# Final norm bound behind the activations of the last expert, its stores on GpSimd's queue, and six way-down pieces multiplied unsplit

## The chip, the core and the metric

One core of a Trainium2 chip runs the whole program. The metric is the device time of one execution in microseconds (us); lower is better. The kernel before was timed three times: median 2451.87 us (2450.3 to 2453.91).

## The reference

Two transformer blocks are computed in float32 on 1024 tokens of width D = 1024. Only the end of the second block matters here: an expert-choice feed-forward layer, its scatter back into the rows, and a last rmsnorm.

```
def expert_choice_ffn(h, w_router, w_gate, w_up, w_down):
    cap = EC_CAPACITY_FACTOR * n // N_EXPERTS            # 128 of 1024 tokens
    aff = jax.nn.softmax((h @ w_router), axis=-1)
    g, idx = lax.top_k(jnp.swapaxes(aff, 1, 2), cap)     # each of 16 experts picks its tokens
    xs = jax.vmap(lambda hb, ib: hb[ib])(h, idx)
    a = jnp.einsum('becd,edf->becf', xs, w_gate)
    u = jnp.einsum('becd,edf->becf', xs, w_up)
    y = jnp.einsum('becf,efd->becd', silu(a) * u, w_down) * g[..., None]
    out = jax.ops.segment_sum(y.reshape(-1, d), flat, num_segments=bsz * n)
...
x = x + gt2 * expert_choice_ffn(h2, w_router, w_gate, w_up, w_down)
return rmsnorm_2(x, g_final)      # x * rsqrt(mean(x*x) + EPS) * g_final
```

A token may be picked by several experts, so the rows of x are complete only when every expert that holds them has been added.

## The kernel before

**The expert stage.** It is the last 600 us. Sixteen experts e (0 to 15) are each cut into four quarters c4, which makes 64 steps i = 4e + c4. A step needs two gate/up pieces of the weights (called gu 2i and gu 2i+1 here) and one way-down piece (d i), 1 MB each. `pipelined` runs three stages one step apart: `ex_gu(s)`, the gate/up products and the silu; `ex_T(s-1)`, the transposes of the 128x256 activation; `ex_down(s-2)`, the way-down products into `py`, which gathers an expert's 128 rows over its four steps.

**Split products.** A float32 weight half is split into two parts: ACT casts it (`wh`, L1521) and DVE subtracts (`wl`, L1522). Each product is then three matmuls (`mm3`, L187 to L189). One step has 24 of them for gate/up and 12 for way-down. Where `whole` is true (before: i = 63 alone) the way-down product is one float32 matmul on the weight as it was loaded (L1741, two records each, eight in a step), with no cast, no `wl`, and a plain copy `af` in place of `ah` and `al`.

**Weights in a ring.** The loaded weights live in 17 slots of 1 MB. `raw_tile` (L1479) walks over the slots' pools in a fixed turn; a pool has 1, 2 or 4 slots. A slot can be loaded again once the last `wl` of its old weight is done on DVE. All loads go through SP's queue, in the order in which the program's scheduler put them; a load that waits holds up all behind it. Each engine works through its own queue in the same way.

**Rows and the final norm.** When an expert's four steps are done, its rows `ys` are scaled by the gate and `gt2` and added into `x3_d` in DRAM by an indirect DMA of GpSimd (L1752). Behind the scatter of expert 14 the last three way-down pieces are loaded (held back by the small copies of L1498), then `final_rows` (L1757) loads `g_final` (`gfin`) and all of x3 in eight tiles of 128 rows (`x3t`, two in a slot), squares them on ACT (`jk`, L168), takes the power on GpSimd (`rrstd`, L164), scales on DVE (L1777) and stores on SP's queue (L1778). The rows of expert 15 are gathered first (`xg`, L1765), get their last addition and norm at the very end (L1788 to L1795), and overwrite their places in `out` by an indirect DMA of GpSimd (L1796), which waits for all other stores.

**What sets the order.** The program is written in the order above; a scheduler that simulates the engines then decides each queue's order and which slot of a pool a tile gets. `tc.issue_after(x)` keeps what is written in it behind instruction x.

Of the kernel before, what the change touches and what calls it, by code (L numbers as in the profile page):

```python
# [6 lines left out]
F32 = mybir.dt.float32  # L7
# [53 lines left out]
ONORM = (26, 29)  # L61
MORE = 2
XSB = 3
LASTN = 3
OH = 1
KV0 = 1
D1S = 3
# [27 lines left out]
def tile_two_blocks(ctx, tc, A, out):  # L95
# [1574 lines left out]
    with TP(name="exg", bufs=2, space=PSUM) as psg, \  # L1670
# [12 lines left out]
        def ex_gu(i, _):  # L1683
# [20 lines left out]
            if c4 == 3 and e + 1 < NE:  # L1704
                x_T(e + 1)
            sg = ex.tile([P, 2, P], F32, name="sg", tag="sg").rearrange("p j c -> p (j c)")
            nc.scalar.activation(sg, pg[:, 0:256], AF.Silu)
            nc.vector.tensor_tensor(out=sg, in0=sg, in1=pg[:, 256:512], op=ALU.mult)
            return sg

        def ex_T(i, ac):
            whole = i == 4 * NE - 1
            pT = pst.tile([P, 4, P], F32, name="pT", tag="tp")
            for j in range(2):
                nc.tensor.transpose(pT[:, j, :], ac[:, j * P:(j + 1) * P], ident)
            if whole:
                af = ex.tile([P, 2, P], F32, name="af", tag="sg")
                nc.scalar.copy(af, pT[:, 0:2, :])
                return af, None
            ah = exa.tile([P, 2, P], F32R, name="ah", tag="ah")  # L1720
            al = exb.tile([P, 2, P], F32R, name="al", tag="al", bufs=ALB)
            split(ah, al, pT[:, 0:2, :])
            return ah, al

        def ex_down(i, a):
            e, c4 = divmod(i, 4)
            whole = i == 4 * NE - 1
            ah, al = a
            if c4 == 0:
                pys[e] = psy.tile([P, D], F32, name="py", tag="y")  # L1730
# [28 lines left out]
        def final_rows():  # L1759

            i_ = ROWS.index("g_final_2")
            last["g"] = ex.tile([P, D], F32, name="gfin", tag="xs", bufs=XSB)
            nc.sync.dma_start(last["g"], A["rows"][i_:i_ + 1, :].partition_broadcast(P).rearrange("p o n -> p (o n)"))
            last["x"] = ex.tile([P, D], F32, name="xg", tag="xs", bufs=XSB)
            nc.gpsimd.indirect_dma_start(out=last["x"], out_offset=None, in_=x3_d,  # L1765
                                         in_offset=bass.IndirectOffsetOnAxis(ap=xT[NE - 1][2], axis=0))
            for u in range(NT // 2):
                xt = raw_tile("x3t")
                for j in range(2):
                    t = 2 * u + j  # L1770
                    x3 = xt[:, j * D:(j + 1) * D]
                    nc.sync.dma_start(x3, x3_d[trow(t), :])
                    jk = ex.tile([P, D], BF16, name="jk", tag="hot", bufs=1)
                    ss = stat.tile([P, 1], F32, name="ss", tag="ss")
                    sumsq(x3, ss, jk)
                    r = rstd_of(ss, 1, D)
                    nc.vector.scalar_tensor_tensor(out=x3, in0=x3, scalar=r, in1=last["g"], op0=ALU.mult, op1=ALU.mult)  # L1777
                    nc.sync.dma_start(out[trow(t), :], x3)  # L1778
# [5 lines left out]
        sq = stat.tile([P, 2], F32, name="ssl", tag="ssl")  # L1784
        jk = ex.tile([P, D], BF16, name="jk", tag="hot", bufs=1)
        for nh in range(2):
            c = slice(nh * 512, nh * 512 + 512)
            nc.vector.scalar_tensor_tensor(out=ys[:, c], in0=pys[NE - 1][:, c], scalar=xT[NE - 1][3], in1=gt2[:, c],  # L1788
                                           op0=ALU.mult, op1=ALU.mult)
            nc.vector.tensor_tensor(out=ys[:, c], in0=ys[:, c], in1=last["x"][:, c], op=ALU.add)  # L1790
            sumsq(ys[:, c], sq[:, nh:nh + 1], jk[:, c])
        ss = stat.tile([P, 1], F32, name="ss", tag="ss")
        nc.vector.tensor_tensor(out=ss, in0=sq[:, 0:1], in1=sq[:, 1:2], op=ALU.add)
        r = rstd_of(ss, 1, D)
        nc.vector.scalar_tensor_tensor(out=ys, in0=ys, scalar=r, in1=last["g"], op0=ALU.mult, op1=ALU.mult)  # L1795
        nc.gpsimd.indirect_dma_start(out=out, out_offset=bass.IndirectOffsetOnAxis(ap=xT[NE - 1][2], axis=0),  # L1796
                                     in_=ys, in_offset=None)
    for p in reversed(exs):
        p.release()
    rt_pool.release()  # L1800
# [109 lines left out]
```

## Time and profile before

| | us |
|---|---|
| median of 3 runs | 2451.87 (2450.3 to 2453.91) |
| the profiled execution | 2454.56 |
| its span, first to last instruction | 2452.6 |
| TensorE (PE) busy | 2322.0 (95%) |
| VectorE (DVE) busy | 1612.5 (66%) |
| ScalarE (ACT) busy | 1122.5 (46%) |
| GpSimd (POOL) busy | 600.1 (24%) |
| mean granted TensorE clock | 0.978 |

The profiled execution is 1.96 us longer than its span and 2.69 us over the median. Matmul records overlap by some 0.17 us, so the start-to-start distance of two, 0.23 us, is what a 128x512 product takes on PE.

### The profile page before, as it was taken

The numbers are of one execution on the slowest core, as the hardware profiler recorded it, in microseconds if no ns is written. First come the engines' busy times: TensorE is split into PE (matmuls) and PEld (weight loads), VectorE is DVE, ScalarE is ACT, GpSimd is POOL, SyncE is SP. The second block draws the span as 40 slices with busy tenths as digits, with TensorE's granted clock in tenths as the row PEclk, the third lists the DMA queues.
The fourth block names the chain that finished last, engine by engine and source line by source line (L and its number), as shares of the span: only waits on it lengthen the run. The fifth ranks groups of instructions, "written<-read, shape, count | busy, mean of one in ns | idle before, by whom it ended". The sixth has DMA issues, their size and how long they took to land. (4 is left out here: it accounts for less than half of the span.)

```text
span 2452.6 us, 33977 instructions
## 1 busy us (share of the span) xinstructions
PE 2322.0 (95%) x12875; PEld 1872.4 (76%) x12875; DVE 1612.5 (66%) x2554; ACT 1122.5 (46%) x1932; POOL 600.1 (24%) x597
## 2 busy tenths in 40 slices
PE   7999999999999999999997999999949999999996
PEld 7977787787878878788876988666737888877774
DVE  4265666457686665554557842575378999999887
ACT  4254566343321222222223421453237887877775
POOL 1100540130000000000005400263154565565512
PEclk9999999999999999999999999999979999999998
DMA  6111003225243331111115320014679999999975
GB/s 199 30 44 61 24 27 98 94 102 163 83 155 103 121 104 61 52 52 43 46 58 141 92 65 26 26 40 147 239 280 337 383 382 381 397 367 360 369 256 214
DMA packets 111031, 381.66 MB, mean 156 GB/s; under 512 B 12215, under 2 KB 19224, under 8 KB 94484
## 3 DMA queue, kind: packets, MB, share of 16 engines
q1 hardware_dynamic: 98980, 344.99, 38.8%
q0 software_dynamic: 6416, 22.97, 4.0%
q10 hardware_dynamic: 5472, 11.54, 1.2%
q8 instruction: 101, 1.65, 0.3%
q14 instruction: 62, 0.51, 0.1%
HBM read 340.08 MB, written 39.37 MB: 155 GB/s over the span
## 5 line engine op out<-in xcount | busy, mean ns | idle before, releaser
L1522 DVE TENSOR_TENSOR wl<-raw,wh 128x1024 fp32r<-128x1024 f32 x380 | 473.9, 1284 | 45.6 <-ACT wh L1521 40.0
L1521 ACT CAST wh<-raw 128x1024 fp32r<-128x1024 f32 x382 | 391.5, 1051 | 67.6 <-PE pg L189 33.7
L171 ACT CAST wh<-raw 128x512 fp32r<-128x512 f32 (+1 forms) x177 | 107.5, 641 | 411.5 <-PE psu L188 225.7
L187 PE MATMUL psu<-hT_hi,wh 128*128 128x512 f32 x704 | 278.6, 396 | 5.8 <-ACT wh L171 5.5
L188 PE MATMUL psu<-hT_lo,wh 128*128 128x512 f32 x704 | 277.8, 395 | 0.0
L189 PE MATMUL psu<-hT_hi,wl 128*128 128x512 f32 x704 | 276.7, 394 | 0.2 <-DVE wl L172 0.2
L164 POOL TENSOR_TENSOR rrstd<-vrstd,neghalf 128x1 f32<-128x1 f32 x51 | 36.1, 730 | 866.5 <-DVE vrstd L161 866.4
L172 DVE TENSOR_TENSOR wl<-raw,wh 128x512 fp32r<-128x512 f32 (+1 forms) x177 | 124.0, 729 | 148.1 <-ACT wh L171 147.9
L888 DVE TENSOR_TENSOR ffn_y<-ffn_y,psd 128x512 f32<-128x512 f32 x160 | 108.6, 684 | 158.0 <-PE psd L189 157.8
L187 PE MATMUL pg<-wh,xh 128*128 128x512 f32 x512 | 204.8, 400 | 5.2 <-ACT xh L171 5.2
L1539 POOL TENSOR_SCALAR hot<-iota,slot 128x128 bf16<-128x128 f32 x112 | 201.2, 2529 | 17.6 <-PE pi L1547 13.2
L188 PE MATMUL pg<-wl,xh 128*128 128x512 f32 x512 | 204.2, 399 | 0.3 <-DVE wl L1522 0.3
L189 PE MATMUL pg<-wh,xl 128*128 128x512 f32 x512 | 202.4, 395 | 0.0
L187 PEld LDWEIGHTS psu<-hT_hi,wh 128*128 128x128 f32 x704 | 133.0, 189 | 38.2 <-ACT wh L171 8.4
L189 PEld LDWEIGHTS psu<-hT_hi,wl 128*128 128x128 f32 x704 | 133.0, 189 | 31.5 <-DVE wl L172 1.1
L188 PEld LDWEIGHTS psu<-hT_lo,wh 128*128 128x128 f32 x704 | 133.1, 189 | 29.9
L187 PE MATMUL psd<-wh,acth 128*128 128x512 f32 x352 | 139.9, 398 | 3.3 <-DVE ffn_y L888 2.6
L188 PE MATMUL psd<-wl,acth 128*128 128x512 f32 x352 | 139.1, 395 | 0.0
L189 PE MATMUL psd<-wh,actl 128*128 128x512 f32 x352 | 138.1, 395 | 0.0
L187 PEld LDWEIGHTS pg<-wh,xh 128*128 128x128 f32 x512 | 96.6, 189 | 25.8 <-ACT xh L171 7.1
L188 PEld LDWEIGHTS pg<-wl,xh 128*128 128x128 f32 x512 | 96.7, 189 | 24.5 <-DVE wl L1522 5.7
L189 PEld LDWEIGHTS pg<-wh,xl 128*128 128x128 f32 x512 | 96.5, 189 | 18.9
(497 smaller groups left out, 5390.0 us busy)
## 6 DMA issues: line engine op xcount, KB each, us to landing
raw<-in_w_gu SPq DMA_DIRECT2D x128, 1024.0 KB
raw<-in_w_down SPq DMA_DIRECT2D x64, 1024.0 KB
wa<-in_w_ada SPq DMA_DIRECT2D x48, 512.0 KB
raw<-in_w_up SPq DMA_DIRECT2D x88, 256.0 KB
raw<-in_w_down SPq DMA_DIRECT2D x44, 256.0 KB
raw<-in_w2t SPq DMA_DIRECT2D x36, 256.0 KB
xt<-in_x SPq DMA_DIRECT2D x16, 512.0 KB
wor<-in_w_out SPq DMA_DIRECT2D x32, 256.0 KB
```

Of the source, the lines that this page charges most:

```text
L164: nc.gpsimd.tensor_tensor(out=r, in0=v, in1=neghalf[:, :n], op=ALU.pow)
L171: nc.scalar.copy(hi, src)
L172: nc.vector.tensor_tensor(out=lo, in0=src, in1=hi.bitcast(F32), op=ALU.subtract)
L187: nc.tensor.matmul(ps, lh, rh, start=start, stop=False)
L188: nc.tensor.matmul(ps, lh, rl, start=False, stop=False)
L189: return nc.tensor.matmul(ps, ll, rh, start=False, stop=stop)
L888: nc.vector.tensor_tensor(out=yt, in0=yt, in1=ps, op=ALU.add)
L1521: nc.scalar.copy(wh, raw[:, sl])
L1522: (eng or nc.vector).tensor_tensor(out=wl, in0=raw[:, sl], in1=wh.bitcast(F32), op=ALU.subtract)
L1539: nc.gpsimd.tensor_scalar(hot[:, t, :], iota1, slot_of[e][:, t, :], None, op0=ALU.is_equal)
```

## The change

`LASTN` and the held loads go. `WHOLE = 6` makes the way-down products of i = 58 to 63 unsplit. The scatter-add of expert 13 is now the last indirect addition: right behind it in the program GpSimd's queue gathers the rows of expert 14 and loads the eight `x3t` tiles, and SP's queue loads `gfin`. `gfin` and the four pairs of `x3t` take five turns of the weight ring there. The pairs' norms (`final_rows(u)`) are bound behind the silu of i = 60, 61, 62 and 63, and they store through GpSimd's queue. The rows of experts 14 and 15 are added in SBUF (`add_rows`), normed (`norm_rows`) and written over their places in `out`; those of expert 14 are also written to `x3_d` without addition, and the rows of expert 15 gathered behind that write.

```
-LASTN = 3
+WHOLE = 6
+FROWS = {58: 0, 59: 1, 60: 2, 61: 3}
...
-            nc.scalar.activation(sg, pg[:, 0:256], AF.Silu)
+            last["gu"] = nc.scalar.activation(sg, pg[:, 0:256], AF.Silu)
...
-            whole = i == 4 * NE - 1
+            whole = i >= 4 * NE - WHOLE
...
                 if e < NE - 2:
                     nc.scalar.activation(ys, py, AF.Copy, scale=xT[e][3])
                     nc.gpsimd.tensor_tensor(out=ys, in0=ys, in1=gt2, op=ALU.mult)
+                    nc.gpsimd.indirect_dma_start(out=x3_d, out_offset=idx, in_=ys, in_offset=None, compute_op=ALU.add)
+                    if e == NE - 3:
+                        last["x"] = rows_of(e + 1)
+                        gn = raw_tile("gfin")
+                        last["g"], last["n"] = gn[:, 0:D], gn[:, D:2 * D]
+                        nc.sync.dma_start(last["g"], ...)
+                        last["t"] = [raw_tile("x3t") for _ in range(NT // 2)]
+                        for t in range(NT):
+                            nc.gpsimd.dma_start(last["t"][t // 2][:, t % 2 * D:t % 2 * D + D], x3_d[trow(t), :])
                 else:
-                    nc.vector.scalar_tensor_tensor(out=ys, in0=py, scalar=xT[e][3], in1=gt2, ...)
-                nc.gpsimd.indirect_dma_start(out=x3_d, ..., compute_op=ALU.add)
-                if e == NE - 2:
-                    while order:
-                        fetch(nc.sync, ys if len(order) <= LASTN else None)
-                    final_rows()
+                    add_rows(e, ys)
+                    nc.gpsimd.indirect_dma_start(out=x3_d, out_offset=idx, in_=ys, in_offset=None)
+                    last["x"] = rows_of(e + 1)
+                    last["y"] = ys
+            if i in FROWS:
+                with tc.issue_after(last["gu"].ins):
+                    final_rows(FROWS[i])
+            if i == 4 * NE - 3:
+                norm_rows(NE - 2, last["y"], last["n"])
...
+        def final_rows(u):
+            xt = last["t"][u]
+            for j in range(2):
...
+                sumsq(x3, ss, jk)
+                r = rstd_of(ss, 1, D)
+                nc.vector.scalar_tensor_tensor(out=x3, in0=x3, scalar=r, in1=last["g"], op0=ALU.mult, op1=ALU.mult)
+                nc.gpsimd.dma_start(out[trow(t), :], x3)
...
+        add_rows(NE - 1, ys)
+        norm_rows(NE - 1, ys, ys)
```

**SP's queue, the last weights.** The first two rows of each piece are the pieces that stand first in the stretch; in the kernel before, `raw_21352` is gu 116, `raw_21654` d 59, and the next five are gu 124, gu 125, d 60, gu 126 and gu 127, then `gfin` and d 61.

```order
L1503 DMA raw_21352<-in_w_gu 128x2048 [waits DMAHW4_49,DVE_49]
L1503 DMA raw_21374<-in_w_gu 128x2048 [waits DMAHW5_49,DVE_49]
...
L1500 DMA raw_21654<-in_w_down2 128x2x1024 [waits DMAHW7_49,DVE_49]
L1503 DMA raw_21679<-in_w_gu 128x2048 [waits DMAHW0_49,DVE_49]
L1503 DMA raw_21681<-in_w_gu 128x2048 [waits DMAHW1_49,DVE_49]
L1500 DMA raw_21683<-in_w_down2 128x2x1024 [waits DMAHW2_49,DVE_49]
L1503 DMA raw_21685<-in_w_gu 128x2048 [waits DMAHW3_49,DVE_49]
L1503 DMA raw_21687<-in_w_gu 128x2048 [waits DMAHW4_49,DVE_49]
```

In the changed kernel `raw_21446` is gu 118, `raw_21666` d 59, `raw_21368` gu 116, `raw_21390` gu 117, `raw_21423` d 56, `raw_21803` gu 127, `raw_21833` d 61, `raw_21870` d 62, `raw_21703` gu 124, `raw_21725` gu 125, `raw_21756` d 60, `raw_21781` gu 126 and `raw_21876` d 63.

```order
L1504 DMA raw_21446<-in_w_gu 128x2048 [waits DMAHW5_49,DVE_49]
...
L1501 DMA raw_21666<-in_w_down2 128x2x1024 [waits DMAHW5_49,DVE_49]
L1504 DMA raw_21368<-in_w_gu 128x2048 [waits DMAHW6_49]
L1504 DMA raw_21390<-in_w_gu 128x2048 [waits DMAHW7_49]
L1501 DMA raw_21423<-in_w_down2 128x2x1024 [waits DMAHW0_49]
L1504 DMA raw_21803<-in_w_gu 128x2048 [waits DMAHW6_49,DMAHW1_49,DVE_49]
L1501 DMA raw_21833<-in_w_down2 128x2x1024 [waits DMAHW7_49,DMAHW2_49,DVE_49]
L1501 DMA raw_21870<-in_w_down2 128x2x1024 [waits DMAHW3_49,DMAHW0_49,DVE_49]
L1504 DMA raw_21703<-in_w_gu 128x2048 [waits DMASW7_49,DMAHW4_49,DMASW6_49,DVE_49]
L1504 DMA raw_21725<-in_w_gu 128x2048 [waits DMAHW5_49,DMAHW4_49,DVE_49]
L1501 DMA raw_21756<-in_w_down2 128x2x1024 [waits DMASW3_49,DMASW2_49]
L1504 DMA raw_21781<-in_w_gu 128x2048 [waits DMAHW5_49,DVE_49]
```

gu 116, gu 117 and d 56 moved from the head of the stretch to behind d 59. gu 124 now waits for two DMAs of GpSimd's queue (DMASW7 and DMASW6, the two stores of the first `x3t` pair) and gu 125 for the landing of gu 124 (DMAHW4) and a DVE instruction: by the program's addresses gu 124, gu 125 and gu 126 lie one after another in the one slot in which the first `x3t` pair lay. The pool of four slots that they come from also holds `gfin` and two more `x3t` pairs; d 60 lies in the slot of the second pair, whose two stores are DMASW3 and DMASW2.

**DVE's queue, around the products' parts of gu 124.** Before, in the stretch of gu 118 (`raw_21430`) and d 57 (`raw_21500`), which is like every other:

```order
L1522 TENSOR_TENSOR wl_21433<-raw_21430,wh_21432 128x1024 [waits DMAHW7_49,Activation_49]
L1708 TENSOR_TENSOR sg_21396<-sg_21396,pg_21351 128x256 [waits Activation_49]
L1522 TENSOR_TENSOR wl_21437<-raw_21430,wh_21436 128x1024 [waits Activation_49]
L1522 TENSOR_TENSOR wl_21455<-raw_21452,wh_21454 128x1024 [waits DMAHW0_49,Activation_49]
L172 TENSOR_TENSOR al_21403<-pT_21399,ah_21402 128x256 [waits PE_49]
L1522 TENSOR_TENSOR wl_21459<-raw_21452,wh_21458 128x1024 [waits Activation_49]
L1522 TENSOR_TENSOR wl_21503<-raw_21500,wh_21502 128x1024 [waits DMAHW1_49,Activation_49]
```

In the changed kernel `x3t_21355` is the first pair, `x3t_21356` the second, `ys_21672` the rows of expert 14, and `sg_21658` belongs to i = 61:

```order
L1809 SCALAR_TENSOR_TENSOR x3t_21355<-x3t_21355,rrstd_21609,gfin_21353 128x1024 [waits DMASW7_49,Pool_49]
L1785 SCALAR_TENSOR_TENSOR ys_21672<-py_21422,gate_20743,mod5_15976 128x512 [waits DMASW3_49,DMASW4_49,DMASW1_49,PE_49]
L1785 SCALAR_TENSOR_TENSOR ys_21672<-py_21422,gate_20743,mod5_15976 128x512
L1787 TENSOR_TENSOR ys_21672<-ys_21672,xg_21351 128x512 [waits DMASW5_49,DVE_49]
L1787 TENSOR_TENSOR ys_21672<-ys_21672,xg_21351 128x512 [waits DVE_49]
L1709 TENSOR_TENSOR sg_21658<-sg_21658,pg_21613 128x256 [waits Activation_49]
L162 TENSOR_SCALAR vrstd_21687<-ss_21685 128x1 [waits Activation_49]
L1809 SCALAR_TENSOR_TENSOR x3t_21356<-x3t_21356,rrstd_21689,gfin_21353 128x1024 [waits DMASW0_49,Pool_49]
L162 TENSOR_SCALAR vrstd_21696<-ss_21694 128x1 [waits Activation_49]
```

The norm of the second `x3t` pair now stands on DVE between the multiplication behind the silu of i = 61 and the two `wl` of gu 124, which come next behind the second scaling of that pair.

**GpSimd's queue, behind the first pair's stores.** Before, the powers follow each other, with no DMA between them:

```order
L1765 DMA xg_21700<-x3_d_94,idx_21094 128x1024 [waits DMASW5_49]
L164 TENSOR_TENSOR rrstd_21709<-vrstd_21707,neghalf_86 128x1 [waits DVE_49]
L164 TENSOR_TENSOR rrstd_21719<-vrstd_21717,neghalf_86 128x1 [waits DVE_49]
L164 TENSOR_TENSOR rrstd_21730<-vrstd_21728,neghalf_86 128x1 [waits DVE_49]
L164 TENSOR_TENSOR rrstd_21740<-vrstd_21738,neghalf_86 128x1 [waits DVE_49]
```

In the changed kernel the write of expert 14's rows (L1764) and the gather of expert 15's (L1776) stand among them:

```order
L1810 DMA out_0<-x3t_21355 128x1024 [waits DMASW7_49,DVE_49]
L1764 DMA x3_d_94<-ys_21672,idx_20741 1024x1024 [waits DMASW3_49,DMASW2_49,DMASW4_49,DMASW1_49,DMASW5_49,DMASW0_49,DVE_49]
L165 TENSOR_TENSOR rrstd_21689<-vrstd_21687,neghalf_86 128x1 [waits DVE_49]
L1776 DMA xg_21682<-x3_d_94,idx_21094 128x1024 [waits DMASW0_49,PE_49]
L1810 DMA out_0<-x3t_21356 128x1024 [waits DVE_49]
L165 TENSOR_TENSOR rrstd_21698<-vrstd_21696,neghalf_86 128x1 [waits DVE_49]
L1810 DMA out_0<-x3t_21356 128x1024 [waits DVE_49]
```

The power for the second half of the second pair (`rrstd_21698`) stands behind that gather, and the gather waits for the landing of the write (DMASW0).

## Rows read from the trace of the kernel before

**Rows 1.** Page, part 1: busy us (share), instructions of each engine.
```profile
PE 2322.0 (95%) x12875; PEld 1872.4 (76%) x12875; DVE 1612.5 (66%) x2554; ACT 1122.5 (46%) x1932; POOL 600.1 (24%) x597
```
**Rows 2.** Chain that ended last: start, us, what.
```profile
2443.03 2.60 DMA out<-x3t
```
**Rows 3.** Windows: us, busy of each engine, PE clock, DMA share, GB/s.
```profile
225.00:227.00 2.00, 2.00 (x6) 1.59 (x5) 0.69 (x1) 0.00 (x0) 0.00 (x0) 0.50 0.65 181
...
2370.00:2400.00 30.00, 28.36 (x129) 22.41 (x128) 27.16 (x28) 23.18 (x29) 4.58 (x2) 1.00 0.17 37
...
2410.00:2420.00 10.00, 9.43 (x43) 7.36 (x42) 7.67 (x9) 6.22 (x8) 5.03 (x5) 1.00 0.88 267
2420.00:2430.00 10.00, 9.28 (x36) 6.28 (x35) 6.41 (x10) 6.67 (x12) 1.12 (x2) 1.00 1.03 410
...
2436.00:2438.00 2.00, 0.00 (x0) 0.00 (x0) 2.00 (x3) 1.94 (x6) 1.07 (x2) 0.50 0.92 375
```
**Rows 4.** Timeline of SP's queue: start, us of issue, what.
```profile
2362.42 3.10 SPq L1503 DMA_DIRECT2D raw<-in_w_gu  x2
...
2411.06 2.42 SPq L1500 DMA_DIRECT2D raw<-in_w_down  x3
```
**Rows 5.** Timeline of ACT, the last 90 us.
```profile
2364.23 1.05 ACT L1521 CAST wh<-raw 128x1024 fp32r<-128x1024 f32 x1 [0.33 <-PE pg L189]
...
2374.90 0.38 ACT L1707 ACTIVATE sg<-pg 128x256 f32<-128x256 f32 x1 [1.06 <-PE pg L189]
...
2394.17 0.38 ACT L1707 ACTIVATE sg<-pg 128x256 f32<-128x256 f32 x1 [0.31 <-PE pg L189]
...
2418.26 1.05 ACT L1521 CAST wh<-raw 128x1024 fp32r<-128x1024 f32 x1 [2.74 <-DMA raw<-in_w_down]
...
2420.83 1.05 ACT L1521 CAST wh<-raw 128x1024 fp32r<-128x1024 f32 x1 [0.30 <-DMA raw<-in_w_down]
...
2425.87 1.06 ACT L168 ACTIVATE jk<-x3t 128x1024 bf16<-128x1024 f32 x1 [2.77 <-DMA x3t<-x_d]
...
2436.63 0.63 ACT L168 ACTIVATE jk<-ys 128x512 bf16<-128x512 f32 x1
```
**Rows 6.** Timeline of DVE, the last 90 us.
```profile
2377.04 2.35 DVE L1522 TENSOR_TENSOR wl<-raw,wh 128x1024 fp32r<-128x1024 f32 x2
...
2427.90 1.28 DVE L1777 SCALAR_TENSOR_TENSOR x3t<-x3t,rrstd,gfin 128x1024 f32<-128x1024 f32 x1 [0.69 <-POOL rrstd L164]
...
2433.12 1.40 DVE L1788 SCALAR_TENSOR_TENSOR ys<-py,gate,mod 128x512 f32<-128x512 f32 x2
...
2434.50 0.68 DVE L1790 TENSOR_TENSOR ys<-ys,xg 128x512 f32<-128x512 f32 x1
```
**Rows 7.** Timeline of POOL, the last 90 us.
```profile
2415.85 2.04 POOL L1765 DMA_INDIRECT xg<-x_d,idx  x1 [2.87 <-DMA x_d<-ys,idx]
2427.29 0.57 POOL L164 TENSOR_TENSOR rrstd<-vrstd,neghalf 128x1 f32<-128x1 f32 x1 [9.40 <-DVE vrstd L161]
...
2446.43 1.05 POOL L1796 DMA_INDIRECT out<-ys,idx  x1 [2.67 <-DMA out<-x3t]
```
**Rows 8.** Timeline of PE: the last products.
```profile
2427.20 0.40 PE L189 MATMUL py<-wh,al 128*128 128x512 f32 x1
2427.43 3.62 PE L1741 MATMUL py<-raw,af 128*128 128x512 f32 x8
```
**Rows 9.** DMAs issued by GpSimd: count, KB, median us from issue to landing.
```profile
ffn_y<-x_d POOLq DMA_DIRECT2D x8, 512.0 KB, 5.6
...
x_d<-ys,idx POOLq DMA_INDIRECT x15, 10.0
...
out<-ys,idx POOLq DMA_INDIRECT x1, 3.4
```
**Rows 10.** Groups by line: issues of L949 (ns), landing of L1426 (half-MB stores).
```profile
L949 POOL DMA_DIRECT2D ffn_y<-x_d x8: 877/882/940, 1295.7 to 1353.3; - x8
...
DMA to landing us min/median/max: 2.9/5.3/7.7
```

More of the change, by code (lines that the diff above doesn't have):

```diff
@@ L1726, in ex_down @@
             e, c4 = divmod(i, 4)
-            whole = i == 4 * NE - 1
+            whole = i >= 4 * NE - WHOLE
             ah, al = a
@@ L1759, in final_rows @@
[L1759 to L1778, printed above, removed]
@@ new lines, in ex_down @@
+                    nc.gpsimd.indirect_dma_start(out=x3_d, out_offset=idx, in_=ys, in_offset=None, compute_op=ALU.add)
[3 more added lines that the diff above has]
+                        last["g"], last["n"] = gn[:, 0:D], gn[:, D:2 * D]
+                        i_ = ROWS.index("g_final_2")
+                        nc.sync.dma_start(last["g"],
+                                          A["rows"][i_:i_ + 1, :].partition_broadcast(P).rearrange("p o n -> p (o n)"))
+                        last["t"] = [raw_tile("x3t") for _ in range(NT // 2)]
+                        for t in range(NT):
+                            nc.gpsimd.dma_start(last["t"][t // 2][:, t % 2 * D:t % 2 * D + D], x3_d[trow(t), :])
+                else:
+                    add_rows(e, ys)
+                    nc.gpsimd.indirect_dma_start(out=x3_d, out_offset=idx, in_=ys, in_offset=None)
+                    last["x"] = rows_of(e + 1)
+                    last["y"] = ys
@@ new lines, in ex_down, with rows_of @@
+            if i in FROWS:
[3 more added lines that the diff above has]
+                norm_rows(NE - 2, last["y"], last["n"])
+        def rows_of(e):
+            xg = ex.tile([P, D], F32, name="xg", tag="xs", bufs=XSB)
+            nc.gpsimd.indirect_dma_start(out=xg, out_offset=None, in_=x3_d,
+                                         in_offset=bass.IndirectOffsetOnAxis(ap=xT[e][2], axis=0))
+            return xg
@@ new lines, in add_rows @@
+        def add_rows(e, ys):
+            last["sq"] = stat.tile([P, 2], F32, name="ssl", tag="ssl")
+            jk = ex.tile([P, D], BF16, name="jk", tag="hot", bufs=1)
+            for nh in range(2):
+                c = slice(nh * 512, nh * 512 + 512)
+                nc.vector.scalar_tensor_tensor(out=ys[:, c], in0=pys[e][:, c], scalar=xT[e][3], in1=gt2[:, c],
+                                               op0=ALU.mult, op1=ALU.mult)
+                nc.vector.tensor_tensor(out=ys[:, c], in0=ys[:, c], in1=last["x"][:, c], op=ALU.add)
+                sumsq(ys[:, c], last["sq"][:, nh:nh + 1], jk[:, c])
@@ new lines, in norm_rows @@
+        def norm_rows(e, ys, to):
+            ss = stat.tile([P, 1], F32, name="ss", tag="ss")
+            nc.vector.tensor_tensor(out=ss, in0=last["sq"][:, 0:1], in1=last["sq"][:, 1:2], op=ALU.add)
+            r = rstd_of(ss, 1, D)
+            nc.vector.scalar_tensor_tensor(out=to, in0=ys, scalar=r, in1=last["g"], op0=ALU.mult, op1=ALU.mult)
+            nc.gpsimd.indirect_dma_start(out=out, out_offset=bass.IndirectOffsetOnAxis(ap=xT[e][2], axis=0),
+                                         in_=to, in_offset=None)
@@ L1780, in tile_two_blocks @@
         pipelined(4 * NE, ex_gu, ex_T, ex_down)
         ys = ex.tile([P, D], F32, name="ys", tag="xs", bufs=XSB)
[L1784 to L1797, printed above, removed]
+        add_rows(NE - 1, ys)
+        norm_rows(NE - 1, ys, ys)
```

10 lines of the change are left out of this document (6 added, 4 removed).

## Prediction

> **What bounds the kernel now.** I read the page's first part, then the windows over the last 90 us, the queues of SP, ACT, DVE and GpSimd there, the end of the chain of waits, and the landing times of GpSimd's DMAs. PE is busy 95% of the span [rows 1]. In the expert stage all three compute engines are nearly full: in the 30 us from 2370, PE is busy 28.4, DVE 27.2 and ACT 23.2 us, while the DMA engines stand at 0.17, because almost every weight already lies in its slot; SP issues its last ring load at 2365.1 (the second of the pair that starts at 2362.42 and takes 3.10) [rows 3, 4]. The reader is to see that a load is free there as long as it is issued many steps ahead, and that weights loaded late are what PE ends up waiting for: d 61, issued at 2411.06, is cast at 2418.26 after ACT stood 2.74 us for it [rows 4, 5]. The last matmul ends at 2431.05 (2427.43 + 3.62) [rows 8]; the remaining 21.5 us are norms, stores, and the last write, issued at 2446.43, 6.17 us before the span's end [rows 7].
>
> **The change, part by part.** Times are on the clock of the profiled execution, whose span is 2452.6; it took 2454.56, 1.96 over its span, and 2.69 over the median of 2451.87. I carry the difference in the span over to the median.
>
> *Unsplit products.* Eight unsplit records take 3.62 us with the overlap of the last, so 3.45 from start to start (0.17 less, the difference between the 0.40 us record and its 0.23 us spacing); twelve split ones take 12 x 0.23 = 2.8 [rows 8]. Five more such steps cost PE 5 x 0.65 = 3.2 us, and take 10 casts of 1.05 from ACT and 10 `wl` of 1.18 from DVE [rows 5, 6]. That helps only where DVE or ACT is late; below PE waits for weights, so I count the 3.45 in and nothing for the relief.
>
> *gu 116 late.* The five slots for `gfin` and `x3t` push twelve weights into the other slots, and on SP gu 116, gu 117 and d 56 now stand behind d 59. d 59 waits for the slot and the `wl` that before let the last ring load go, so gu 116 goes at about 2365.5, where before it was cast at 2364.23 [rows 4, 5]. Price of one lone 1 MB load: not shown. Below: a lone half MB store takes 2.60 [rows 2], and a MB more in a row 2.57 (casts 2418.26 and 2420.83) [rows 5], half of it 1.28, so 3.9. Above: 7.2, d 61 from issue to cast, beside two others and a scatter [rows 4, 5]. Nearest is the half MB load `ffn_y`, 5.6, less its issue of 0.88 on GpSimd, 4.7 [rows 9, 10]; I take 5.0. d 59 lands at 2370.2, gu 116 at 2372.8, gu 117 at 2375.4. Two casts (2.1) of gu 117, a `wl` (1.2) and six products (1.4) later the silu of i = 58 comes at about 2380.4, 5.5 after the 2374.90 of before [rows 5]. From there to the silu of i = 60 PE has 72 split products (16.6: two steps of gate/up and d 56 and d 57), d 58 unsplit (3.45) and about 1.5 of transposes and hand-overs, 21.6: 2402.0 against 2394.17, 7.8 later [rows 5].
>
> *The first pair's norm and stores.* Loading `x3t` early lies in the empty stretch from 2370 [rows 3] and I cost it at nothing; it is landed long before 2402. On ACT behind the silu (0.38) come a copy of the same kind (0.35), a square (1.25 with its read-out), a cast (1.05) and the second square; from a square's start to its scaled row 3.3 us pass (2425.87 to 2429.18) [rows 5, 6]. So the second store goes at 2402.0 + 0.38 + 0.35 + 1.25 + 1.05 + 3.3 + 0.2 = 2408.5. Stores of half a MB by GpSimd landed in 2.9, to 7.7, median 5.3 [rows 10]; I take 5.3: 2413.8.
>
> The Trainium skill ("DMA: Bandwidth & Descriptors", "Anatomy of one DMA — SWDGE (gpsimd) path") fits a GpSimd DMA as 2.0 us plus its bytes over 436e3 per us, an estimate of 3.2 for half a MB. The row of 5.6 and the median of 5.3 do not agree with it, only the fastest, 2.9, does; by the page the store lands 2.1 earlier and the forecast below would be 2468.
>
> *Three weights through one slot.* gu 124 waits for those two stores. It then lands at 2418.8, and its `wl` on DVE stand behind the scaling of the second pair's second half, whose power stands on GpSimd behind the gather that waits for the landing of expert 14's write. The rows of expert 14 are ready at about 2413.1: 24 gate/up products (5.5), d 59 unsplit (3.45) and hand-overs (0.7) behind the silu of i = 60 make 2411.7, d 59 ends six products (1.4) before that, and two steps on DVE follow, 1.40 and 2 x 0.68 [rows 6]. The write lands 3.4 later by the one plain indirect write [rows 9], by the scatter-adds 10.0; I take 3.4, the same kind: 2416.5. Gather 2.04, store 0.88, power 0.57, scaling 1.28 [rows 6, 7, 10] and hand-overs 0.2: 2421.5. Two `wl` (2.35): slot free at 2423.9 (without the block 2418.8 + 1.05 + 2.35 = 2422.2; with 10.0 for the write 2430.5). gu 125: 5.0 to land, 1.05, 2.35, 8.4 in all [rows 5, 6]: 2432.4. gu 126 lands at 2437.4, its second `wl` ends at 2440.8, its last six products at 2442.3. Nothing hides this: all other weights but d 60 to d 63 and gu 127 are used up, and products of later pieces stand behind on PE's queue.
>
> *The rest.* d 61, gu 127, d 62 and d 63: 3 x 3.45 + 2.8 = 13.15 [rows 8], and about 2.2 for transposes, silu and copies between them (silu 0.38, DVE and copy about 0.4 each, twice, part hidden): last product at 2457.6.
>
> *The tail.* It loses the eight norms and their stores and keeps expert 15: multiplication 1.40, addition 1.36 [rows 6], from a half square (0.63 for 1.06 [rows 5]) to the scaled row 2.9, sum of squares 0.2, hand-overs 0.5: 6.4. The last write goes at 2464.0; with 6.17 behind it as before [rows 7] the span is 2470.2, that is 17.6 longer: 2469.5, rounded to **2470**.
>
> **The rivals.**
>
> *A. The same chain with PE at the lower clock.* In the two turns PE has some 6 us of work in each 8.4 or less. Before, PE stood still from 2431.05, and in 2436 to 2438 the granted clock was 0.50, the lower of its levels (1.2 GHz); in 225 to 227 PE, busy all the time, also had 0.50 [rows 3]. The last 13.15 us of products would lose between nothing and 13; about 6 makes 2476, and with the upper prices (10.0 for the write, 7.7 for a store, 7.2 for a load) 2486. For it: PE stands still from about 2411.7 to 2419. Against it: in the turns it has work again.
>
> *B. The turns are short.* gu 116 lands soon (3.9 for a load, 1.1 earlier), the store in 2.9 (2.4), no block (1.7), three loads at 3.9 (3.3 less), gaps between the last products 1.0 instead of 2.2 and other hand-overs 1.0 less: 10.7 in all, 2459; with half of the 5.5 of gu 116 hidden 2456.
>
> *C. The change gains.* The mechanism: gu 124 to gu 126 land before PE needs them, because the first pair is normed and stored while PE still has work, so the tail decides alone. The last product then comes at 2431.05 + 3.2, less the stand of some 1.3 us at 2416 to 2430 (PE busy 9.43 and 9.28 of 10 [rows 3]), 2433.0; with a tail of 6.4 + 6.17 the span is 2445.6, 7 shorter: **2445**. It decides from the point where the three turns end before the products of i = 61, at about 2412. Against it: they begin with a store that cannot be issued before the silu of i = 60, 2394.17 at the earliest, and need at least 6.4 + 2.9 + 3 x 7.3 behind it, so 2425 at the best.
>
> *D. Gain and loss cancel.* Late weights cost what the shorter tail (21.5 against 12.6) gives back: within 5 us of before. That needs B's prices and gu 116 hidden entirely.
>
> **How the numbers follow.** Forecast 0.60, A 0.17, B 0.10, C 0.07, D 0.06. The forecast's own range is 2462 to 2478. The range for 8 in 10 runs from B's lower end, 2456, to short of A's upper end, 2484. No change that can be measured is within 0.2%, 4.9 us. Faster is C, 0.07; same is D and a sliver of B, 0.07; slower 0.86.
>
> **What would show it.** In the changed profile: casts of gu 116 at about 2373, and PE idle before them; the silu of i = 60 near 2402; SP's load of gu 124 at about 2414, waiting for a DMA of `out<-x3t`; three loads of gate/up on SP 8 to 9 us apart, ACT's casts waiting for `raw<-in_w_gu`, and PE busy well under 8 of 10 from 2412 to 2442; last matmul near 2458, the last write some 6.4 behind it. The prediction is wrong if gu 124 is issued before 2405, if two of the three loads overlap, or if the last matmul comes before 2445.

## The result, and the profile after

| | before | after |
|---|---|---|
| median, us | 2451.87 (2450.3 to 2456.19, 5 runs) | 2481.99 (2472.35 to 2485.29, 5 runs) |
| ratio, 95% interval | | 1.0106 [1.009, 1.0122] |
| span of the profiled execution | 2452.6 | 2483.5 |
| silu of i = 57 to the last product | 65.2 | 98.4 |
| last product to the end | 21.55 | 13.5 |

The change costs 1.1%, some 26 us by the ratio; the medians differ by 30. The 2482 lies inside the range of 2456 to 2484, which the rivals' prices had widened, and on the forecast's side; but it is 12 us over the forecast's 2470, and 4 over the end of the forecast's own range, 2478.

Up to the silu of i = 57 the two programs do the same work; it comes at 2365.84 before and 2371.62 after. Of this difference 4.2 us have grown by 1858 in code that did not change, and in the repeat below it is 1.7. Over the other kernels below, the same silu comes between 2.2 us earlier and 6.4 later than before, and in the one with the gather first, whose program has the same order up to there, 0.1 later. I take it as scatter between executions, so all kernels below are measured from that silu to the end of the span: 86.8 us before, 111.9 after, 25.1 more. The forecast made it 17.6.

The first part of the page of the changed kernel answers to [rows 1]; PE's share is about the same, so the page alone does not show where 25 us went:

```profile
PE 2338.4 (94%) x12855; PEld 1877.2 (76%) x12855; DVE 1601.0 (64%) x2545; ACT 1112.8 (45%) x1926; POOL 606.3 (24%) x613
```

The windows do (columns as in [rows 3]):

```profile
2370.00:2380.00 10.00, 5.46 (x25) 4.02 (x24) 2.25 (x4) 3.29 (x5) 3.94 (x2) 0.95 0.98 403
2380.00:2390.00 10.00, 9.54 (x31) 7.36 (x31) 8.27 (x8) 6.86 (x8) 2.63 (x3) 0.71 1.02 336
...
2420.00:2430.00 10.00, 1.05 (x3) 0.30 (x2) 1.50 (x3) 4.98 (x9) 3.51 (x5) 0.67 0.58 165
2430.00:2440.00 10.00, 4.87 (x11) 3.46 (x11) 3.56 (x3) 0.00 (x0) 0.63 (x2) 0.65 0.82 284
2440.00:2450.00 10.00, 7.36 (x16) 4.25 (x16) 2.36 (x2) 2.41 (x3) 0.00 (x0) 0.66 0.49 182
2450.00:2460.00 10.00, 9.76 (x36) 6.24 (x35) 7.37 (x9) 6.10 (x10) 1.69 (x3) 1.00 0.23 83
```

There are two holes: 4.5 us of PE near 2375, and 16.7 us in the 30 us from 2420. Before, PE was busy 9.43 and 9.28 of 10 in the windows from 2410 and 2420 [rows 3]. SP's queue and ACT name them (start, us, what, and in brackets the idle time ahead and its releaser):

```profile
2371.40 0.93 SPq L1504 DMA_DIRECT2D raw<-in_w_gu  x2
...
2420.29 13.71 SPq L1504 DMA_DIRECT2D raw<-in_w_gu  x2
2435.73 0.38 SPq L1501 DMA_DIRECT2D raw<-in_w_down  x1
2444.54 0.33 SPq L1504 DMA_DIRECT2D raw<-in_w_gu  x1
```
```profile
2378.46 1.99 ACT L1522 CAST wh<-raw 128x1024 fp32r<-128x1024 f32 x2 [2.85 <-DMA raw<-in_w_gu]
...
2388.73 0.38 ACT L1708 ACTIVATE sg<-pg 128x256 f32<-128x256 f32 x1 [0.32 <-PE pg L190]
...
2409.90 0.39 ACT L1708 ACTIVATE sg<-pg 128x256 f32<-128x256 f32 x1 [0.54 <-PE pg L190]
...
2426.44 1.99 ACT L1522 CAST wh<-raw 128x1024 fp32r<-128x1024 f32 x2 [3.39 <-DMA raw<-in_w_gu]
...
2441.08 1.99 ACT L1522 CAST wh<-raw 128x1024 fp32r<-128x1024 f32 x2 [12.64 <-DMA raw<-in_w_gu]
...
2449.58 2.95 ACT L1522 CAST wh<-raw 128x1024 fp32r<-128x1024 f32 x3 [6.51 <-DMA raw<-in_w_gu]
```

The first hole is gu 116, issued at 2371.40 behind d 59 and cast at 2378.46. The second is gu 124, gu 125 and gu 126, one behind the other through one slot: issued at 2420.29, 2433.65 (the second of the row of 13.71, whose issue ends it) and 2444.54, cast at 2426.44, 2441.08 and 2449.58. The first turn, 13.4 us, is the longest, and GpSimd and DVE show why:

```profile
2417.21 0.57 POOL L1810 DMA_DIRECT2D out<-x3t  x1 [1.62 <-DVE x3t L1809]
2419.73 1.02 POOL L1764 DMA_INDIRECT x_d<-ys,idx  x1 [1.94 <-DVE ys L1787]
...
2427.79 1.04 POOL L1776 DMA_INDIRECT xg<-x_d,idx  x1 [5.09 <-DMA x_d<-ys,idx]
...
2429.43 0.60 POOL L165 TENSOR_TENSOR rrstd<-vrstd,neghalf 128x1 f32<-128x1 f32 x1
...
2476.19 1.02 POOL L1796 DMA_INDIRECT out<-ys,idx  x1 [1.61 <-DVE ys L1795]
```
```profile
2430.07 1.28 DVE L1809 SCALAR_TENSOR_TENSOR x3t<-x3t,rrstd,gfin 128x1024 f32<-128x1024 f32 x1 [5.98 <-POOL rrstd L165]
2431.27 2.35 DVE L1523 TENSOR_TENSOR wl<-raw,wh 128x1024 fp32r<-128x1024 f32 x2
```

The gather stands for the landing of expert 14's write, the power behind it for the gather, the scaling on DVE for the power, and the `wl` of gu 124, cast by 2428.4, for the scaling. The chain that ended last has the same links, with the durations of the DMAs (start, us, what):

```profile
2419.73 7.30 DMA x_d<-ys,idx
...
2433.65 7.40 DMA raw<-in_w_gu
...
2444.54 4.94 DMA raw<-in_w_gu
...
2466.31 3.71 PE py L1742 x8
```

And the `x3t` stores, grouped as in [rows 9], landed faster than [rows 10] led me to take (the last number is the median of the eight; the two of the first pair took 2.9 each):

```profile
out<-x3t POOLq DMA_DIRECT2D x8, 512.0 KB, 3.1
```

### The profile page after: what moved, and what is told of

Read it like the earlier page. It is cut to its first block, busy times and chain, and to the rows that moved or that the text cites. A ratio compares the mean times of both kernels' runs of the same rounds, so it can differ in the third digit from the quotient of the medians.

```text
span 2483.5 us, 33899 instructions
## 1 busy us (share of the span) xinstructions
PE 2338.4 (94%) x12855; PEld 1877.2 (76%) x12855; DVE 1601.0 (64%) x2545; ACT 1112.8 (45%) x1926; POOL 606.3 (24%) x613
## 5 line engine op out<-in xcount | busy, mean ns | idle before, releaser
L1523 DVE TENSOR_TENSOR wl<-raw,wh 128x1024 fp32r<-128x1024 f32 x370 | 461.1, 1283 | 67.1 <-ACT wh L1522 61.1
L1522 ACT CAST wh<-raw 128x1024 fp32r<-128x1024 f32 x372 | 380.6, 1051 | 94.6 <-PE pg L190 41.1
L189 PE MATMUL pg<-wl,xh 128*128 128x512 f32 x512 | 209.5, 409 | 5.4 <-DVE wl L1523 5.4
L188 PEld LDWEIGHTS psu<-hT_hi,wh 128*128 128x128 f32 x704 | 133.3, 189 | 40.2 <-ACT wh L172 10.4
```

What stands on the lines that cost most here:

```text
L188: nc.tensor.matmul(ps, lh, rh, start=start, stop=False)
L189: nc.tensor.matmul(ps, lh, rl, start=False, stop=False)
L1522: nc.scalar.copy(wh, raw[:, sl])
L1523: (eng or nc.vector).tensor_tensor(out=wl, in0=raw[:, sl], in1=wh.bitcast(F32), op=ALU.subtract)
```

## Experiments

Each is measured by its ratio to the kernel before on the same chip and by two spans of its profile: from the silu of i = 57 to the last product, and to the end (before 65.2 and 86.8; after 98.4 and 111.9).

**The change again.**

> The changed kernel once more, to see what of its 30 us lies behind the silu of i = 57, the last point before which the program is the same. The first profile had 111.9 us from there to the end (before 86.8) and 5.8 us ahead of it. Theory (only the last stretch is slower, the 5.8 us are how executions of this program scatter): 110 to 113 us from there to the end again, another number ahead of it, median 2475 to 2482. Rival (the change also slows the stages ahead of it): 5 us or more ahead of it again.

Median 2481.61 (2475.09 to 2485.64, 6 runs) against 2454.89, ratio 1.0105 [1.0084, 1.0125]; 99.6 and 113.1. The loss is there again, with the same two holes. Two executions of one kernel thus differ by 1.2 us in these spans.

**Only the unsplit products, on the kernel before.**

```
-            whole = i == 4 * NE - 1
+            whole = i >= 4 * NE - 6
```

> The kernel before with only the six unsplit steps (58 to 63). Theory: PE is the bound there, five steps at 0.65 us more make 3 us: 2455, 89 to 90 us from the silu of i = 57 to the end. Rival (ACT and DVE, which lose 10 casts and 10 subtractions, are what PE waits for): no slower than before, 86 to 87 us.

2456.35 (11 runs) against 2453.2, ratio 1.0011 [1.0001, 1.0021]; 71.1 and 87.2. The last product comes 5.85 later, but the tail is 5.5 shorter, since the norms of `x3t` on the other engines go on beside PE. So the end is nearer to the rival's 86 to 87 than to the 89 to 90 that I expected. One row of its PE queue shows 2.64 of the 5.85; the other 3.2 are what five steps at 0.65 make:

```profile
2427.01 8.80 PE L1742 MATMUL py<-raw,af 128*128 128x512 f32 x16 [2.64 <-POOL rrstd L165]
```

(PE waits there for the copy `af`, which ACT makes at 2426.56, behind two squares of `x3t`; the releaser in the bracket is inferred.) So this part of the change costs some 0.1%, and the 25 us are elsewhere.

**All weights fetched ahead of the norm's slots.** In the changed kernel, `gfin` and `x3t` take their turns of the ring only after the last weight has been given one.

```
                     if e == NE - 3:
                         last["x"] = rows_of(e + 1)
+                        while order:
+                            fetch(nc.sync)
                         gn = raw_tile("gfin")
```

> The changed kernel with one thing moved: all weights that are left are asked for before gfin and the four x3t pairs take their slots of the ring. Theory (the loss is in the slots: gu 116 late, and gu 124 to gu 126 one after another in one slot): nothing waits for weights any more, the five unsplit steps cost about 3 us, the tail is about 13.5 us instead of 21.5; from the silu of i = 57 to the end of the span about 79 us (before 86.8, changed kernel 111.9), so about 2444. Rival 1 (the norms and stores put among the last products, or the stores on GpSimd's queue, cost the time): still over 2465. Rival 2 (the unsplit products): a few us over 2452.

2462.05 (2455.73 to 2470.25, 8 runs) against 2453.2, ratio 1.0036 [1.0023, 1.0049]; 67.5 and 93.3. Both holes are gone: the last product comes 31 us sooner than after, 2.3 later than before, and PE has hardly a gap where they were:

```profile
2370.00:2380.00 10.00, 9.75 (x44) 7.63 (x43) 8.26 (x9) 8.57 (x11) 3.39 (x2) 1.00 0.91 350
...
2420.00:2430.00 10.00, 10.00 (x38) 6.57 (x37) 4.81 (x9) 4.51 (x13) 1.12 (x2) 1.00 0.00 0
```

I expected 2444 and missed by 18, mostly because a tail of 25.8 took their place. On DVE the rows of expert 14 are now added only behind the silu product of i = 62, on GpSimd the write follows at 2438.38 behind powers and stores, and expert 15's addition waits for the gather:

```profile
2421.55 1.40 DVE L1787 SCALAR_TENSOR_TENSOR ys<-py,gate,mod 128x512 f32<-128x512 f32 x2
...
2452.18 1.29 DVE L1789 TENSOR_TENSOR ys<-ys,xg 128x512 f32<-128x512 f32 x2 [5.88 <-DMA xg<-x_d,idx]
```
```profile
2438.38 1.53 POOL L1766 DMA_INDIRECT x_d<-ys,idx  x1 [0.19 <-issue]
...
2444.36 1.51 POOL L1778 DMA_INDIRECT xg<-x_d,idx  x1 [0.30 <-issue]
```

**Three weights fetched first.** As above, with three turns (`for _ in range(3)` in place of `while order`), which puts gu 116, gu 117 and d 56 back in time.

> The changed kernel with only gu 116, gu 117 and d 56 asked for ahead of gfin and x3t. gu 116 is in time; by the program's addresses gu 126 then comes behind gu 124 in one slot, and gu 127 behind the first pair's stores, but gu 124 and gu 125 are early. Theory: the 8 us at gu 116 go, and of the chain one turn is left, partly hidden: 92 to 98 us from the silu of i = 57 to the end. Rival (gu 116's delay was only a shift that later stages absorb): over 100 us.

2457.86 (10 runs) against 2454.89, ratio 1.0012 [1.0, 1.0024]; 75.9 and 89.3. The end comes 2.7 us sooner than the lower end of what I expected. The one turn that the expectation left is there: gu 127, behind the first pair's stores, is late (14.6 us from the silu of i = 62 to that of i = 63, 10.1 before). But the three turns also shift the ring, so that gu 124 and gu 125 come early. So this does not price the lateness of gu 116 alone.

**Gather ahead of the write.** This leaves out expert 14's part in the rows that expert 15 shares with it.

```
+                    last["x"] = rows_of(e + 1)
                     nc.gpsimd.indirect_dma_start(out=x3_d, out_offset=idx, in_=ys, in_offset=None)
-                    last["x"] = rows_of(e + 1)
```

> The changed kernel with the gather of expert 15's rows issued ahead of the write of expert 14's rows (so a token that both hold lacks expert 14's part in it). The power for the second pair then no longer waits on GpSimd for the write's landing of 7.3 us. Theory (this wait holds gu 124's wl and so the whole chain of three loads): 3 to 5 us faster than the changed kernel, 107 to 109 us from the silu of i = 57 to the end. Rival (gu 124's landing sets the turn, the wait is beside it): no change, 111 to 112 us.

2479.12 (4 runs) against 2453.2, ratio 1.0107 [1.0092, 1.0122]; 97.0 and 110.5. The turn of gu 124 is 10.1 instead of 13.4 (row of 10.40 on SP's queue): the block by the gather is worth 3.3. But the gather now stands ahead of the second store of the first pair:

```profile
2410.16 2.07 POOL L1776 DMA_INDIRECT xg<-x_d,idx  x1 [0.18 <-issue]
2412.24 0.58 POOL L1810 DMA_DIRECT2D out<-x3t  x1
```

From the silu of i = 60 to the issue of gu 124 it takes 13.4 instead of 10.4, which gives the gain back. Of the span, 1.4 is left, about what the change and its repeat differ by (1.2), and the ratio is that of the change. So the wait did hold gu 124's `wl`, as the theory had it, but the time came out as the rival's: no gain.

**Stores on SP's queue, as before.** `nc.gpsimd.dma_start(out[trow(t), :], x3)` becomes `nc.sync.dma_start(...)`.

> The changed kernel with the pairs' stores on SP's queue instead of GpSimd's; the slots stay, and gu 124 still waits for the first pair's stores. On GpSimd the powers of the second pair come to stand ahead of the gather. Theory (which queue stores is not what costs): 108 to 112 us from the silu of i = 57 to the end, within 4 us of the changed kernel. Rival (GpSimd's stores hold up its queue): 6 us or more faster.

2471.71 (2468.56 to 2475.47, 4 runs) against 2454.89, ratio 1.0065 [1.0041, 1.0088]; 93.3 and 106.1, 5.8 less than after; by the medians it is 9.9 less than the repeat of the change, on the same chip. The theory, that the queue does not matter, missed. The scheduler now puts the second pair's powers ahead of the gather, and gu 124, gu 125 and gu 126 go 9.4 and 10.1 apart instead of 13.4 and 10.9:

```profile
2415.60 0.34 SPq L1504 DMA_DIRECT2D raw<-in_w_gu  x1
...
2425.01 0.34 SPq L1504 DMA_DIRECT2D raw<-in_w_gu  x1
...
2435.08 0.33 SPq L1504 DMA_DIRECT2D raw<-in_w_gu  x1
```

The queue of the stores is thus worth between a quarter (by the spans) and nearly four tenths (by the medians) of the loss. The spans show where most of it comes from: the two turns are 4.8 shorter together, 4.0 of it in that of gu 124, through what stands behind the gather. Three turns through one slot stay.

**Norms two steps earlier.** `FROWS = {56: 0, 57: 1, 58: 2, 59: 3}`.

> The changed kernel with the four pairs' norms bound behind the silu of i = 58 to 61 instead of 60 to 63; the pairs' slots come free two steps earlier, and by the program's addresses gu 124, gu 125 and gu 126 then lie in three slots; gu 116 stays late. Theory: the wait for three loads in a row goes (about 21 us), that for gu 116 (about 8) stays: 2459 to 2463, 90 to 92 us from the silu of i = 57 to the end. Rival (the time is lost by norms and stores among the products): no faster than 2475.

2468.9 (4 runs) against 2453.2, ratio 1.0064 [1.0049, 1.0078]; 88.2 and 101.6, where I expected an end at 90 to 92. The slot is free in time, but ACT now stands at the first square for the loading of `x3t`, behind which stand the casts of the next weights:

```profile
2392.27 1.06 ACT L169 ACTIVATE jk<-x3t 128x1024 bf16<-128x1024 f32 x1 [9.11 <-DMA x3t<-x_d]
```

In its window from 2390 to 2400 PE is busy 4.02 us of 10, at a clock of 0.50. I had not asked when `x3t` could be there at the earliest: behind the scatter of expert 13 and the gather of expert 14's rows.

**Weights first, and expert 14's rows ahead.** The kernel of the third experiment, with the `wl` and products of i = 62 bound behind expert 14's sums on DVE, and the norms behind the gather on GpSimd.

```
+            if i == 4 * NE - 2:
+                with tc.issue_after(last["add"].ins):
+                    gu_mm()
...
-                with tc.issue_after(last["gu"].ins):
+                with tc.issue_after(last["gu"].ins), tc.issue_after(last["xg"].ins):
```

> As e1 (all weights asked for ahead of gfin and x3t), and the order forced in two places: gu 124's wl stand behind the addition of expert 14's rows on DVE, and the norms of the pairs behind the gather of expert 15's rows on GpSimd and ACT's silu. In e1 that gather went out at 2444.36 and landed 7.7 us later, behind the last product, so the tail was 26.5 us. Theory (what is left in e1 over the kernel before is that late write and gather): the tail is 13 to 14 us, 80 to 82 us from the silu of i = 57 to the end, 2445 to 2448. Rival (the norms beside the last products hold up ACT and DVE, and PE): the last product over 70 us behind the silu of i = 57 (before 65.2), no gain over before.

2453.82 (12 runs) against 2454.89, ratio 0.9996 [0.9984, 1.0007], no difference; 70.6 and 85.7. The rival held. The tail is repaired, 15.1 instead of 25.8, but from the silu of i = 61 to that of i = 62 it takes 13.2 (8.5 before). DVE stands idle, and then makes four `wl` in a row behind the sums:

```profile
2404.08 0.42 DVE L1715 TENSOR_TENSOR sg<-sg,pg 128x256 f32<-128x256 f32 x1 [7.87 <-ACT sg L1714]
...
2408.97 4.62 DVE L1523 TENSOR_TENSOR wl<-raw,wh 128x1024 fp32r<-128x1024 f32 x4
```

**The same, with only d 63 unsplit.** `WHOLE = 1`.

> The kernel of e12 (all weights fetched ahead of the norm slots, expert 14's rows added ahead of the next weight halves) with only d 63 unsplit, as before. Theory (the unsplit products cost PE their 5 x 0.65 = 3.2 us wherever weights are on time, and their relief of 10 casts and 10 weight halves goes to engines that could have done them): the last product 67 to 68 us behind the silu of i = 57 (70.6 in e12), the end 82 to 84 behind it (85.7), time 2450 to 2452. Rival (the relief is needed, since ScalarE and VectorE are full beside the norms): the last product 70.5 or more, the end 85.7 or more, 2454 or more.

2459.5 (10 runs) against 2455.24, ratio 1.0021 [1.0009, 1.0032]; 78.8 and 92.3. The rival held, and by far: splitting five products again costs 8.3 us up to the last product (5.3 in the time by the medians), where I expected to gain 3. Their `wl` stand between the scalings of `x3t` on DVE:

```profile
2436.34 2.47 DVE L1817 SCALAR_TENSOR_TENSOR x3t<-x3t,rrstd,gfin 128x1024 f32<-128x1024 f32 x2
2438.73 1.22 DVE L1523 TENSOR_TENSOR wl<-raw,wh 128x1024 fp32r<-128x1024 f32 x1
```

PE waits 3.06 and 1.20 for such `wl` in its last products. Beside norms, the unsplit products pay.

**The norms in other steps.** Six unsplit again, `FROWS = {58: (0,), 60: (1,), 61: (2, 3)}`, and the casts of i = 61 bound behind the squares of the first pair. A number in `FROWS` names a whole pair here, not a half as the expectation says: pair 0 is bound behind the silu of i = 60, pair 1 behind that of i = 62, pairs 2 and 3 behind that of i = 63.

> The kernel of e12 with the norms of both pairs spread over other steps: the first half of pair 0 in the step of i = 58, its second half in that of i = 60, both halves of pair 1 in that of i = 61, and the squares of the first bound ahead of the casts of the gate/up weights of i = 61. Six unsplit products as in the change. Theory (the 13.2 us from the silu of i = 61 to that of i = 62 in e12, 8.5 before, come from four norms that fall into one step of ScalarE and VectorE): that step is 9.5 or less, the last product 66 to 67 behind the silu of i = 57, the end 80 to 82, time 2447 to 2449. Rival (the work only moves to the next step, ScalarE and VectorE are full everywhere): the end 85 or more behind the silu, 2453 or more.

2459.94 (12 runs) against 2455.24, ratio 1.002 [1.0008, 1.0032]; 75.4 and 92.3. A miss: the step from the silu of i = 61 to that of i = 62 took 9.2, as expected, but the one ahead of it, from the silu of i = 60, took 19.5 (9.1 in the kernel it was made from). Four casts, done a step ahead until then, stand behind the squares:

```profile
2401.25 1.06 ACT L169 ACTIVATE jk<-x3t 128x1024 bf16<-128x1024 f32 x1
...
2403.49 3.87 ACT L1522 CAST wh<-raw 128x1024 fp32r<-128x1024 f32 x4
```

It is my binding that cost this, so whether norms in separate steps alone would gain stays open.

**That, with three products unsplit.** `WHOLE = 3`.

> The kernel of e14 with three products unsplit (d 61 to d 63) instead of six. Theory (the other three, d 58 to d 60, cost PE 3 x 0.65 = 1.95 us and give back nothing): the end 78 to 80 us behind the silu of i = 57, 1.5 to 2 less than e14, time 2445 to 2447. Rival (their 6 casts and 6 weight halves fall into the steps in which ScalarE and VectorE are full): the end as in e14 or later.

2463.05 (8 runs) against 2455.24, ratio 1.0036 [1.0024, 1.0049]; 80.1 and 97.0. The rival again: with three more split products the last product comes 4.7 later (3.1 in the time by the medians, and the two intervals overlap).

**Half the weights free.** The kernel with weights first and expert 14's rows ahead (six unsplit, norms as in the change), with only the second half of i = 62 bound.

```
-            if i == 4 * NE - 2:
-                with tc.issue_after(last["add"].ins):
-                    gu_mm()
+            gu_mm(0)
+            if i == 4 * NE - 2:
+                with tc.issue_after(last["add"].ins):
+                    gu_mm(1)
```

> The kernel of e12 with only gu 125 of the weights of i = 62 bound behind expert 14's sums, and gu 124 free to go ahead of them. Theory (in e12 VectorE stood idle for 7.9 us before the silu product of i = 61 and only then made four weight halves in a row, 4.6 us, behind the sums; two of them fit into the idle time): the silu of i = 62 comes 10 to 11 us behind that of i = 61 (13.2 in e12, 8.5 before), the last product 67.5 to 68.5 behind the silu of i = 57 (70.6 in e12), the end 82.5 to 83.5 (85.7), time 2450 to 2452, below the kernel before by what can just be measured. Rival (the norms' squares and scales of the same step fill what is won): 12.5 or more from silu to silu, the end 85 or more, 2453 or more.

2450.63 (2448.48 to 2458.36, 12 runs) against 2455.4, ratio 0.9983 [0.9969, 0.9997]: the only kernel here that is faster than before, by 0.17%. The last product comes as expected, 68.3 behind the silu of i = 57, and PE is full, where the kernel it was made from had 8.27 of 10 in the second of these windows (its silu of i = 57 comes 1.6 later):

```profile
2400.00:2410.00 10.00, 10.00 (x36) 6.07 (x35) 6.29 (x9) 5.99 (x9) 0.00 (x0) 1.00 0.01 2
2410.00:2420.00 10.00, 10.00 (x38) 6.97 (x37) 7.54 (x13) 9.17 (x18) 3.41 (x5) 1.00 0.20 81
```

But the silu of i = 62 is no earlier (13.9 behind that of i = 61): on ACT it stands behind two squares, and PE does the products of i = 63 meanwhile. And the profile's end is 86.1 behind the silu of i = 57, as in the kernel it was made from (85.7): the 2.3 us won on PE went into the tail, where DVE still scales `x3t` when expert 15's last product is done at 2431.95:

```profile
2434.14 1.40 DVE L1793 SCALAR_TENSOR_TENSOR ys<-py,gate,mod 128x512 f32<-128x512 f32 x2
```

So its time is the best, but the profile does not show that it beats the kernel it was made from, and the two intervals overlap. Of the 2.8 us by which its span is shorter than that of the kernel before, 2.2 lie ahead of the silu of i = 57.

## Why the prediction came out as it did

The mechanism was right. gu 116 late, gu 124 behind the first pair's stores, three loads through one slot, a block by the write and the gather, a shorter tail: each is a row of the changed profile, and taking the cause away (weights first) takes both holes away. With the 5.78 us of the start taken off, the steps compare so:

| step, us | forecast | measured | adds to the error |
|---|---|---|---|
| gu 116 cast | 2372.8 | 2372.7 | |
| silu of i = 58 | 2380.4 | 2383.0 | +2.5 |
| silu of i = 60 | 2402.0 | 2404.1 | -0.4 |
| second store issued | 2408.5 | 2411.4 | +0.8 |
| gu 124 issued | 2413.8 | 2414.5 | -2.2 |
| gu 124's slot free | 2423.9 | 2427.9 | +3.3 |
| gu 126 issued | 2432.4 | 2438.8 | +2.4 |
| last product ends | 2457.6 | 2464.2 | +0.3 |
| last write issued | 2464.0 | 2470.4 | -0.2 |
| end of the span | 2470.2 | 2477.7 | +1.1 |

By the last row it is 7.5: the changed part costs 25.1 instead of 17.6. (The sign "8 to 9 us apart" for the three loads did not fit that sum, in which they go 10.1 and 8.5 apart; measured were 13.4 and 10.9.) The terms that were mis-sized:

- *The write of expert 14.* "The write lands 3.4 later by the one plain indirect write [rows 9], by the scatter-adds 10.0; I take 3.4, the same kind." It took 7.3. The row that I went by was the last write of the kernel, with nothing beside it; this one runs beside gu 124's load, issued 0.56 us behind it. The other kernels bear that out. In the repeat and the two others where gu 124's load is issued within 0.6 us of it, it took 7.1 to 7.9. Where no weight load is issued near it (the kernels with weights first, and the one with three weights first) it took 3.8 to 4.5, but for the one with the norms in other steps, 7.5, where the issue itself took 4.24; with a load issued 1.1 us ahead of it (norms two steps earlier) it took 5.1. With weights first and expert 14's rows ahead, 4.4:

```profile
2419.01 2.08 POOL L1772 DMA_INDIRECT x_d<-ys,idx  x1 [0.37 <-issue]
2423.70 1.00 POOL L1784 DMA_INDIRECT xg<-x_d,idx  x1 [2.62 <-DMA x_d<-ys,idx]
```

- *gu 125's turn.* "5.0 to land" holds for gu 126, 4.94. gu 125 took 7.40. For its first 2.0 us the last store of the second pair was still under way, and d 60, which waits for that store, was issued 2.1 us behind gu 125. With d 60 0.4 us behind it and that store landed (gather ahead of the write), gu 125 took 5.75. I had both on the lists and did not ask what they do to gu 125's landing; how the 2.4 divide between them is not shown.
- *gu 116.* The landing was right, but in the window from 2380 the granted clock was 0.71, after PE had been busy 5.46 of 10: the products of gu 116 went 0.43 apart, those of gu 117 0.23. Twelve times 0.2 is 2.4, the error of this step. My price for the stand left the clock out.
- *The store.* Taken at 5.3, landed in 2.9. Here the estimate of 3.2 (the Trainium skill, "DMA: Bandwidth & Descriptors", "Anatomy of one DMA — SWDGE (gpsimd) path") was nearer than the median of another stage, and the -2.2 hid part of the other errors. The eight `x3t` loads of the same size and queue had a median of 10.7; they were issued some 0.55 apart, while the two stores had no load beside them. So that fit agrees with the stores only.
- *The rest.* From gu 126 on, products, hand-overs and tail were within 0.3; ahead of gu 124 they were 0.4 under and 0.8 over. The end behind the last write was 7.3 instead of 6.2.

The remaining gap of the medians, 2482 against the forecast's 2470, is about what the profile has with its start taken off (2477.7) and some 5 us of scatter.

Rival A named the lower clock in the turns, and the windows from 2420 show it: 0.65 to 0.67, between the two levels, with products of the split kind 0.43 us apart instead of 0.23. But there it cost next to nothing, since the 11 or 12 products of a turn still ended before the next weight was there; it had its price only at gu 116. The last products ran at 1.00, not at the lower level that A needed for its 6 us. A's number, 2476 to 2486, came out nearer than mine, mainly by its upper prices, a long landing for the write and for a load; its own mechanism, the clock of the last products, did not come. Rivals B, C and D fell: no turn was under 10.9.

The forecast took the unsplit products at their cost on PE with no relief. Added to the kernel before, they cost 0.11% [0.01, 0.21]. In the repaired kernel, which has the norms beside the last experts, taking them back costs some 5 us by the medians (4.3 over before instead of 1.1 under it). That the relief "helps only where DVE or ACT is late" was right, but I would have looked for it in the wrong kernel.

What stays open: why executions differ by some 6 us ahead of the changed part (1.6 of the 5.78 come near 2165, where the granted clock was 0.72 in the changed profile's window from 2166 to 2172, and 1.00 in the window from 2162 to 2168 of the kernel before and of the one with the gather first); and the price of gu 116 alone, since each edit that brings it in time shifts the other slots as well.

## What to carry to other kernels

A tile that takes a turn in a ring of weights displaces every weight behind it, and the one that reloads that slot waits for the tile's last reader, a store included: fetch the weights first, in program order, and give the leftover turns to the norm. Here that, with the order of expert 14's rows put right, brought the change back to the time of the kernel before, not clearly below it. When work is pulled from the tail into a full stage, ask for each engine what now stands behind it, above all a GpSimd DMA that waits for another's landing, since the powers, stores and scalings queued behind it hold up the weights. A landing time must come from a row with the same traffic beside it; one from the quiet end of a kernel was here a lower bound.

## What the runs showed that I had not expected

- One write of half a MB by indices (L1764) took 7.3 us to land beside one weight load, where the last one of the kernel before took 3.4 [rows 9].
- One MB of gate/up weights landed in 4.94 us alone and in 7.40 with the end of a store ahead of it and a second MB issued 2.1 us behind it.
- The order on one engine decided more than its load: with four casts bound behind two squares, the step to the silu of i = 61 took 19.5 us (9.0 before), while DVE and ACT were busy 55.3 and 46.2 of the 80 us from 2365. With four `wl` bound behind expert 14's sums, the step to the silu of i = 62 took 13.2 (8.5 before), with both engines at most 71% busy; freeing two of them brought the last product 2.3 us nearer, but that step stayed at 13.9, so there the squares share in it.
